# Encoder layer on one core: the modulation's later dot products run in the attention and beside the whole mLSTM, and pauses stand ahead of three TensorE steps

## The chip, the cores and the metric

The kernel runs on one core of a Trainium2 chip. The metric is the time of one execution on the device in microseconds (us); the profile takes one execution apart. TensorE (PE) multiplies matrices, VectorE (DVE), ScalarE (ACT) and GpSimd (POOL) work element by element, and SyncE (SP) issues nearly all DMA transfers. Every engine carries out its own instructions in the order in which they were written down, and waits at one whose inputs are not ready.

## The reference, cut to what matters

```python
cond = jax.nn.silu(c)                                        # (1, 1024)
mod = cond @ w_ada[l] + b_ada[l]                             # 6 x 1024
sh1, sc1, g1, sh2, sc2, g2 = jnp.split(mod, 6, axis=-1)
h = modulate(rms_norm(x, norm_mix_g[l]), sh1, sc1)           # h * (1 + sc1) + sh1
proj = h @ w_in[l]
q_a, k_a, v_a, qk_m, v_m, o_m, gates = jnp.split(proj, splits, axis=-1)
y_attn = axial_gqa_attention(q_a, k_a, v_a, ...)             # 8 heads of 64, 2 key/value heads, rotary
y_mem = bidirectional_mlstm(qk_m, v_m, o_m, gates, ...)      # 4 heads of 128, convolution of 5 taps ahead
mix = jnp.concatenate([y_attn, y_mem], axis=-1) @ w_out[l]
x = x + g1[:, None, :] * mix
h = modulate(rms_norm(x, norm_ffn_g[l]), sh2, sc2)
ffn = (jax.nn.silu(h @ w_gate[l]) * (h @ w_up[l])) @ w_down[l]
x = x + g2[:, None, :] * ffn
return rms_norm(x, final_norm_g)
```

All inputs are float32, the sequence has 1024 positions, the model 1024 channels, the FFN 2816. The modulation is a product of a vector with a 1024 x 6144 matrix of 24 MB. `sh1` and `sc1` are needed before the projection, `g1` (columns 16 to 23 of `mod`, 128 channels to a column) when the output projection is added to x, `sh2` and `sc2` (24 to 39) at the second norm, and `g2` (40 to 47) at the end of the FFN.

## The kernel before

Activations lie transposed, channels on the 128 partitions. Every large matmul is made of three (lines 298 to 300, `mm3`): weights and activations are split into a high part, rounded to fp32r by ScalarE (`whi`, `hh`), and the rest, made by GpSimd or VectorE (`wlo`, `hl`).

The kernel's own emitter fixes the order of the instructions. `Clock` holds an estimate of each engine's time. `Clock.chain` is a list of steps: each is written down when the one ahead of it should be done by that estimate, so the elementwise engines get their instructions in the order of estimated time. `Clock.streams` walks generators of TensorE work (`Stream`): the main ones go first, the filling ones (`un`, the units of the input projection or later of the output projection) when no main one is ready. TensorE itself never changes the order: a matmul that a chain writes down too early holds up everything behind it until its input is there. Elementwise instructions and DMA issues all go through one helper each (lines 96 and 303).

The stages, one after another:

- First norm and the first tiles of the projection, with the modulation's columns 0 to 15 as full dot products.
- The input projection's units (`IN`): `q_unit` (queries), `conv_unit` (mLSTM queries and keys with their convolution, tiles `xp` and `y`), `chunk_unit` (values, output gates and the mLSTM's gate columns). Beside them run `rope_steps` for the keys and four pairs of query heads, and `gate_steps`, a long chain on VectorE and ScalarE that turns the mLSTM's gates into cumulative sums, maxima and exponentials. Three of their steps are TensorE instructions written down by a chain: `squares` (lines 645 and 651: sums of squares of queries and keys, inputs `sqk` from ScalarE), `columns` (line 908: 16 transposes of the exponentials `T`, from ScalarE) and `spread` (line 922: a matmul that spreads the decay `dexp`, from VectorE, over all partitions). The stage goes on until the fourth pair of query heads is stored and the gates are done.
- Attention: three main streams (`scores`, line 978; `turned`, transposes of the probabilities, line 1010; `values`, line 1029) over 8 heads x 8 blocks of queries, filled with projection units.
- mLSTM: four main streams (`states`, `fronts`, `backs`, `ends`; tiles `mk`, `Cs`, `W`, `num`, `hs`), first filled with what is left of the input projection, then, from the loading of `x1` on, with the output projection (`MIX`). Between the two, the pool `big` and the projection's input are freed, and the tiles of x (`x1p`) take their place.
- Output projection, second norm, FFN.

The modulation's columns 16 to 47 are made late, in 64 half columns: `ada_late` loads one half column of the transposed `w_ada` (128 x 512, 256 KB, tile `ada`) and writes down one VectorE instruction that multiplies it by `cond` and sums along the row into `modacc`; the instruction that reads the sum out (`DVE_READ_ACCUMULATOR`) follows it. It has two buffers and asks for another one only when the one but last should be done by the emitter's estimate. It is called in three places: in the projection stage, at most once per estimated microsecond (`ready`), once ahead of every block of scores, both up to 48, and in the mLSTM (`ck.tick`, at every step of a stream) up to 64. `mod_sum` adds the two halves and the bias.

```python
        def ready():
            if ck.t > t_ada[0]:
                ada_late()
                t_ada[0] = ck.t + 1.0
            return rope_ok[3].done and gates_ok.done and not open_sum[0]
```

## Time and profile before

| | |
|---|---|
| median of 3 runs (lowest to highest) | 1405.2 us (1403.0 to 1405.35) |
| the profiled execution's own time | 1407.29 us |
| its span, first to last instruction | 1405.5 us |
| mean granted TensorE clock | 0.972 |
| busy: PE, DVE, ACT, POOL | 93%, 76%, 47%, 48% of the span |
| half columns on VectorE before 207 us, in 207 to 300, in 507 to 557 | 30, 18, 16 |
| scores of the attention begin; mLSTM's last output is stored | 206.8 us; 674.7 us |

How to read the profile. Times are in us from the span's start, mean durations of single instructions in ns. A line of waits reads: engine, tile and line that waited, the one that released it, us in total, times, longest. A line of stretches gives start and end, length, then busy us and number of instructions for PE, PEld (weight loads of TensorE), DVE, ACT and POOL, the granted TensorE clock (1.00 is full speed), the share of the 16 DMA engines that was busy, and GB/s. In a line of the timeline stand start, duration, engine, line, operation, output and inputs, and in square brackets the idle time ahead of it and what ended it. SPq is SP's own queue, in which DMA issues wait for their buffers. Tile names have no buffer numbers: `ada` is a half column, `T` both the gates' exponentials and the attention's transposed probabilities, `x` the residual stream.

### The profile page before, as it was taken

Reading aid. Unit: us, or ns where it says so; the run is one execution under the profiler, and the core shown is the slowest. Engines: PE = TensorE matmul, PEld = TensorE weight load, DVE = VectorE, ACT = ScalarE, POOL = GpSimd, SP = SyncE. Lnnn points to the kernel's source line nnn. Section 1 sums busy time; section 2 is a strip of 40 time slices with the busy share of each in tenths; the row PEclk is TensorE's granted clock in tenths of the full one; section 3 lists DMA queues with packets and bytes.
Section 4 is the critical chain, followed back from the end, with each engine's and each line's share of the span. In section 5 each row is a group of like instructions: output and inputs, shape, how many; then the busy total and the mean of one; then the engine's idle time right before and its main releaser. Section 6 shows DMA issues by size and latency. Waiting matters only on the chain.

```text
span 1405.5 us, 19481 instructions
## 1 busy us (share of the span) xinstructions
PE 1300.5 (93%) x6594; PEld 1072.1 (76%) x6602; DVE 1065.1 (76%) x1600; ACT 662.9 (47%) x1194; POOL 679.0 (48%) x555
## 2 busy tenths in 40 slices
PE   5789798999999989899996999999999999979997
PEld 2578577889878979777774888888888887757887
DVE  7947979986788848768589886666666654798866
ACT  5454316677666655454476333332332334344463
POOL 5555554545344336577421355454544545545542
PEclk9899989999999999999998999999999999989999
DMA  7446462322122146553552333322332259723324
GB/s 287 165 128 203 135 172 80 108 77 65 38 65 70 35 140 211 188 203 115 196 187 75 113 120 105 107 104 100 110 113 90 71 175 327 275 81 102 93 65 154
DMA packets 103172, 184.40 MB, mean 131 GB/s; under 512 B 11296, under 2 KB 32672, under 8 KB 103072
## 3 DMA queue, kind: packets, MB, share of 16 engines
q1 hardware_dynamic: 89968, 161.06, 36.0%
q10 hardware_dynamic: 13104, 22.10, 4.2%
q8 instruction: 52, 0.85, 0.2%
q14 instruction: 48, 0.39, 0.1%
HBM read 136.19 MB, written 43.25 MB: 128 GB/s over the span
## 4 chain that ended last, share of the span: by engine, by line
PE 61%; DVE 20%; DMA 6%; issue 5%; ACT 3%; POOL 3%; SPq 1%; DVEq 0%; ACTq 0%; POOLq 0%
PE acc L299 15%; PE acc L298 15%; PE acc L300 15%; DVE x L96 3%; PE av L1029 3%; DVE ada L96 3%; DVE sst L96 2%; PE T L1010 2%; DVE PT L96 2%; PE S L978 2%; DVE y L96 1%; PE acct L298 1%; PE acct L300 1%; PE acct L299 1%; DVE wd L96 1%
## 5 line engine op out<-in xcount | busy, mean ns | idle before, releaser
L96 POOL TENSOR_TENSOR wlo<-wst,whi 128x512 fp32r<-128x512 f32 (+2 forms) x196 | 279.5, 1432 | 285.0 <-ACT whi L96 272.9
L96 ACT ACTIVATE whi<-wst 128x512 fp32r<-128x512 f32 (+2 forms) x219 | 131.0, 605 | 125.1 <-POOL wlo L96 25.3
L96 POOL TENSOR_SCALAR P<-P,sst 128x1024 f32<-128x1024 f32 x64 | 88.9, 1392 | 141.1 <-DVE sst L96 106.4
L299 PE MATMUL acc<-x,whi 128*128 128x512 f32 x352 | 140.7, 400 | 5.9 <-DVE x L96 5.9
L96 POOL TENSOR_TENSOR wlo<-wr,whi 128x512 fp32r<-128x512 f32 x56 | 76.9, 1374 | 77.4 <-ACT whi L96 73.9
L298 PE MATMUL acc<-hh,whi 128*128 128x512 f32 x224 | 97.5, 435 | 14.1 <-ACT hh L96 11.8
L298 PE MATMUL acc<-whi,wch 128*128 128x512 f32 x244 | 97.2, 398 | 6.3 <-ACT wch L96 6.3
L96 ACT ACTIVATE P<-S,sst,colq 128x1024 f32<-128x1024 f32 x64 | 77.3, 1207 | 52.4 <-DVE sst L96 47.9
L299 PE MATMUL acc<-hl,whi 128*128 128x512 f32 x224 | 92.4, 412 | 8.2 <-POOL hl L96 4.5
L300 PE MATMUL acc<-whi,wcl 128*128 128x512 f32 x244 | 97.2, 398 | 2.9 <-DVE wcl L96 2.8
L299 PE MATMUL acc<-wlo,wch 128*128 128x512 f32 x244 | 97.0, 398 | 0.6 <-POOL wlo L96 0.5
L96 DVE SCALAR_TENSOR_TENSOR ada<-ada,cond 128x512 f32<-128x512 f32 (+1 forms) x79 | 80.2, 1023 | 18.3 <-DMA ada<-in_w_ada_dram 12.7
L300 PE MATMUL acc<-hh,wlo 128*128 128x512 f32 x224 | 91.5, 409 | 0.0
L96 DVE TENSOR_TENSOR sg<-acc,sg 128x512 f32<-128x512 f32 x67 | 45.4, 687 | 58.8 <-PE acc L300 58.5
L96 ACT ACTIVATE PT<-T 128x512 fp32r<-128x512 f32 x128 | 71.4, 597 | 37.7 <-PE T L1010 36.9
L96 ACT ACTIVATE whi<-wr 128x512 fp32r<-128x512 f32 x60 | 37.9, 632 | 108.1 <-DVE wr L96 50.3
L96 DVE TENSOR_TENSOR PT<-T,PT 128x512 fp32r<-128x512 f32 x128 | 82.8, 681 | 7.2 <-ACT PT L96 7.1
L96 POOL TENSOR_TENSOR wlo<-s,whi 128x512 fp32r<-128x512 f32 x40 | 53.8, 1347 | 70.7 <-ACT whi L96 70.7
L299 PEld LDWEIGHTS acc<-x,whi 128*128 128x128 f32 x352 | 67.0, 190 | 22.3 <-DVE x L96 7.3
L298 PE MATMUL acct<-whi,hh 128*128 128x256 f32 (+1 forms) x256 | 79.4, 310 | 2.5 <-ACT xp L96 1.2
L96 DVE TENSOR_TENSOR wcl<-wd,wch 128x512 fp32r<-128x512 f32 x50 | 48.0, 972 | 42.1 <-ACT wch L96 26.9
L1010 PE MATMUL T<-con,P 128*128 128x128 f32 x512 | 70.3, 275 | 10.2 <-DVE PT L96 7.4
(459 smaller groups left out, 3802.5 us busy)
## 6 DMA issues: line engine op xcount, KB each, us to landing
wr<-in_w_gu_dram SPq DMA_DIRECT2D x66, 256.0 KB, 2.8
ada<-in_w_ada_dram SPq DMA_DIRECT2D x64, 256.0 KB, 3.3
wd<-in_w_d_dram SPq DMA_DIRECT2D x22, 512.0 KB, 7.0
wst<-in_w_gu_dram SPq DMA_DIRECT2D x34, 256.0 KB, 3.1
wst<-act_d SPq DMA_DIRECT2D x33, 256.0 KB, 4.1
ada<-in_w_ada_dram SPq DMA_DIRECT2D x16, 512.0 KB, 5.5
wst<-in_w_o_dram SPq DMA_DIRECT2D x32, 256.0 KB, 4.3
act_d<-sg ACTq DMA_DIRECT2D x31, 256.0 KB, 2.0
```

The source lines that it names most:

```text
L96: return fn(*args, **kw)
L298: nc.tensor.matmul(acc, w[0], x[0], start=first, stop=False)
L299: nc.tensor.matmul(acc, w[0], x[1], start=False, stop=False)
L300: nc.tensor.matmul(acc, w[1], x[0], start=False, stop=last)
L978: nc.tensor.matmul(sp[:, halves(n)], qs[:, j * P:(j + 1) * P], k2[g][m][:, halves(n)], start=m == 0, stop=m == 1)
L1010: nc.tensor.transpose(tp[:, k], Pt[q][:, (4 * b + k) * P:(4 * b + k + 1) * P], ident)
L1029: nc.tensor.matmul(av, va[:, k, h // 4], PT[it][m][:, k], start=(k, m) == (0, 0), stop=(k, m) == (NJ - 1, 1))
```

## The change

The projection stage no longer calls `ada_late`. The attention makes 32 half columns (columns 16 to 31) instead of what was missing of 48. The mLSTM makes the other 32: until the input projection's end in the two buffers of the pool `big`, from then on, once the first tiles of the attention's output are split, in the ring `yat` of the mLSTM's pool (4 buffers, 2 asked for ahead); it goes on through the output projection's filling, and what is missing at the end is made in a closing loop. `cond` lies in the mLSTM's pool. `mod_sum` is called for 16 to 31 before the mLSTM and for 32 to 47, with `sc2`, when all are done. `later(dt)` is a step of a chain that writes nothing down and puts the steps after it off by `dt` us of the emitter's estimate: 2.5 us ahead of `squares`, 6 us ahead of `columns`, 5 us ahead of `spread`.

```diff
--- before.py
+++ after.py
@@ -617,6 +617,12 @@
         va_ok = [Flag(), Flag()]
         rp = []
 
+        def later(dt):
+
+            def wait():
+                ck.fin = ck.now + dt
+            return wait
+
         def rope_steps(i, accs):
 
             is_k = i == 4
@@ -676,7 +682,7 @@
                              lambda t=t, g=g: act.activation(k2[g][0], t, AF.Copy),
                              lambda t=t, g=g: gps.tensor_sub(k2[g][1], t, k2[g][0].bitcast(F32)), flag=k2_ok[g])
 
-            ck.chain(0.0, lambda: evac(0), lambda: evac(1), swap, squares)
+            ck.chain(0.0, lambda: evac(0), lambda: evac(1), swap, later(2.5), squares)
 
         def v_steps(accs):
             vt = bp.tile([P, S], F32, tag="big", name="vt")
@@ -925,26 +931,29 @@
 
             ck.chain(0.5, lambda: rows(0), lambda: rows(1), lambda: None, *[lambda i=i: soft(i) for i in range(3)], logf, mask,
                      *[lambda i=i: scan(i) for i in range(4)], ends, rows_r, rows_hl, inter,
-                     lambda: exps(0), lambda: exps(1), state, lambda: exps(2),
+                     lambda: exps(0), lambda: exps(1), state, lambda: exps(2), later(6.0),
                      *[lambda i=i, b=b: columns(i, b) for i in range(2) for b in range(2)],
-                     lambda: dve.tensor_scalar(cols[:, :, 1], cols[:, :, 1], QK, None, op0=OP.mult), decay, spread,
+                     lambda: dve.tensor_scalar(cols[:, :, 1], cols[:, :, 1], QK, None, op0=OP.mult), decay, later(5.0), spread,
                      lambda: None, flag=gates_ok)
 
         adas = []
         summed = []
 
-        def ada_late(last=48, ahead=2):
+        def ada_late(last=32, ahead=2):
 
             n = len(adas)
             if n == 64 and all(f.done for f in adas[-2:]) and not summed:
                 summed.append(1)
-                mod_sum(40, 48)
+                mod_sum(32, 48)
+                dve.scalar_tensor_tensor(sc2, mod[:, 32:40], 1.0, V("norm_ffn_g", 0, KT), op0=OP.add, op1=OP.mult)
             if n >= last or n >= ahead and not (adas[n - ahead].done and adas[n - ahead].t <= ck.t):
                 return
             j, i = 16 + n // 2, n % 2
-            t = PP["ada"].tile([P, HALF], F32, tag="ada", name="ada", bufs=ahead)
+            t = PP["ada_new"]()
             adas.append(ck.chain(dma(t, w_ada[j][:, halves(i)]), lambda: dve.scalar_tensor_tensor(
                 t, t, 1.0, PP["cond"][:, halves(i)], op0=OP.mult, op1=OP.mult, accum_out=modacc[:, i, j:j + 1])))
+
+        PP["ada_new"] = lambda: PP["ada"].tile([P, HALF], F32, tag="ada", name="ada", bufs=2)
 
 
         NQ = AH * NJ
@@ -1922,12 +1931,7 @@
             rp.append(stp.tile([P, S], F32, tag="x", name="rps", bufs=KT))
             dma(rp[i], rope[i])
 
-        t_ada = [0.0]
-
         def ready():
-            if ck.t > t_ada[0]:
-                ada_late()
-                t_ada[0] = ck.t + 1.0
             return rope_ok[3].done and gates_ok.done and not open_sum[0]
 
         ck.streams([un], stop=ready)
@@ -1939,7 +1943,7 @@
         att_q(0)
         ck.streams([Stream(values()), Stream(turned()), Stream(scores())], [un])
         ck.streams([un], stop=lambda: convs[-1].done and len(convs) == 8 and not open_sum[0])
-        while len(adas) < 48:
+        while len(adas) < 32:
             ck.need(*adas[-2:])
             ada_late()
         ck.need(*adas, *convs, *stores)
@@ -1947,28 +1951,26 @@
         appool.__exit__(None, None, None)
         kvpool.__exit__(None, None, None)
         bp = PP["ada"] = big_open(3)
-        load_cond(bp)
 
 
         def mod_sum(a, b):
             dve.tensor_add(mod[:, a:b], modacc[:, 0, a:b], V("b_ada", a, b - a))
             dve.tensor_add(mod[:, a:b], mod[:, a:b], modacc[:, 1, a:b])
 
-        mod_sum(16, 40)
+        mod_sum(16, 32)
         sc2 = const.tile([P, KT], F32, name="sc2")
-        dve.scalar_tensor_tensor(sc2, mod[:, 32:40], 1.0, V("norm_ffn_g", 0, KT), op0=OP.add, op1=OP.mult)
         mlpool = tc.tile_pool(name="ml", bufs=1)
         mp = mlpool.__enter__()
+        load_cond(mp)
         OPL[:] = mp, 4
         psum_open("ps2", {"acc": ("acc", 2), "acct": ("acc", 2), "tr": ("tr", 1), "U": ("U", 2), "E": ("E", 1),
                           "na": ("na", 1), "ni": ("ni", 1)})
         mem = [Stream(g) for g in (ends(), backs(), fronts(), all_states())]
         ck.tick = lambda: ada_late(64)
         ck.streams(mem, [un], stop=lambda: un.wait is None and all(f.done for v in vo_ok for f in v))
-        while not summed:
-            ck.need(*adas[-2:])
-            ada_late(64)
-        ck.tick = None
+        ck.need(*adas[-2:])
+        PP["ada_new"] = lambda: mp.tile([P, HALF], F32, tag="yat", name="ada", bufs=4)
+        ck.tick = lambda: (0, 0) in Y and all(y[2].done for y in Y[0, 0]) and ada_late(64)
         BIGP[0].__exit__(None, None, None)
         hTpool.__exit__(None, None, None)
         x1p = ctx.enter_context(tc.tile_pool(name="x1", bufs=1, side="right"))
@@ -1980,6 +1982,10 @@
                 ck.at(0.5 + 1.2 * (k + KT * n), lambda k=k, n=n: dma(new_x1(k, n, F32), xT[k][:, halves(n)]))
         ck.streams(mem, [un])
         ck.streams([un], stop=lambda: not open_sum[0])
+        while not summed:
+            ck.need(*adas[-2:])
+            ada_late(64)
+        ck.tick = None
         ck.need(*[f for ring in PP["ring"].values() for f in ring], *[f for y in ym_ok for f in y])
         mlpool.__exit__(None, None, None)
         midpool.__exit__(None, None, None)
```

## The prediction

> **What bounds the kernel now.** First the page: busy shares, then the slices.
>
> ```profile
> PE 1300.5 (93%) x6594; PEld 1072.1 (76%) x6602; DVE 1065.1 (76%) x1600; ACT 662.9 (47%) x1194; POOL 679.0 (48%) x555
> ...
> PE   5789798999999989899996999999999999979997
> ...
> PEclk9899989999999999999998999999999999989999
> ```
>
> TensorE is the bound: it is idle for 105 us of the 1405.5 us span, so an edit pays only by what it takes from TensorE's idle time or from stretches at a lower clock (the 8 of slice 6, 176 to 211 us), or costs by what it adds there. So I cut the span into the stages that the change touches.
>
> ```profile
> 120.00:207.00 87.00, 74.30 (x318) 59.49 (x316) 72.22 (x102) 30.46 (x44) 48.54 (x31) 0.90 0.56 173
> 207.00:300.00 93.00, 84.64 (x543) 72.99 (x542) 90.25 (x156) 60.24 (x102) 46.74 (x30) 1.00 0.35 104
> 300.00:360.00 60.00, 58.96 (x421) 53.44 (x420) 42.51 (x81) 41.99 (x76) 24.44 (x22) 1.00 0.18 53
> 360.00:507.00 147.00, 140.52 (x908) 122.57 (x907) 121.14 (x194) 94.84 (x166) 61.30 (x47) 1.00 0.16 48
> 507.00:557.00 50.00, 45.82 (x340) 43.07 (x343) 31.94 (x92) 26.00 (x69) 25.49 (x43) 1.00 0.70 215
> 557.00:601.00 44.00, 38.39 (x213) 32.54 (x214) 33.81 (x63) 19.89 (x53) 29.67 (x40) 0.92 0.62 208
> 585.00:607.00 22.00, 20.96 (x106) 16.62 (x106) 14.59 (x24) 11.65 (x30) 19.42 (x25) 1.00 1.02 361
> ```
>
> Columns: stretch, length, busy time of PE, PEld, DVE, ACT, POOL, granted clock, DMA share, GB/s. 120 to 207 is the gate and rotary stage beside the projection, 207 to 507 the attention, from 507 the mLSTM. The first row is the poorest: 12.7 us of TensorE idle and a clock of 0.90. The waits in it:
>
> ```profile
> PE T L922 <- DVE dexp L96: 4.7, 1, 4.7
> PE T L908 <- ACT T L96: 4.2, 2, 3.1
> PE ms L651 <- ACT sqk L96: 2.3, 2, 1.8
> PE acc L298 <- ACT xp L96: 1.5, 2, 0.7
> ```
>
> The first three are the steps that get a pause: spread (L922), columns (L908), squares (L651). TensorE stands in order at an instruction whose input ScalarE or VectorE has not finished. The clock:
>
> ```profile
> 136.00:144.00 8.00, 7.48 (x24) 6.16 (x24) 7.92 (x8) 2.18 (x5) 7.81 (x6) 0.57 0.33 99
> 150.00:160.00 10.00, 9.38 (x49) 7.59 (x47) 9.75 (x16) 3.05 (x5) 2.84 (x2) 1.00 0.42 127
> 174.00:185.00 11.00, 9.63 (x32) 8.34 (x33) 4.71 (x21) 0.19 (x2) 5.12 (x3) 0.53 0.60 168
> ```
> ```profile
> 151.84 1.84 PE L651 MATMUL ms<-con,sqk 128*128 128x2 f32 x16
> ...
> 175.95 3.57 PE L651 MATMUL ms<-con,sqk 128*128 128x2 f32 x16
> ```
>
> Right behind the squares' wait (about 135) and the spread's wait (to 175.4) the clock is low. The same 16 matmuls take 1.84 us at 151.84, where nothing was waited for, and 3.57 us behind the spread. Lost: 8 x 0.43 = 3.4 us, and 11 x 0.47 = 5.2 us less half of the 1.37 us in which TensorE was idle there anyway, 4.6 us. Together 8.0 us.
>
> **Where the dot products stand now.** VectorE's groups in 207 to 300 and in 512 to 557, then single tiles with their first and last start:
>
> ```profile
> L96 DVE SCALAR_TENSOR_TENSOR ada<-ada,cond 128x512 f32<-128x512 f32 x18 | 17.1, 950 | 0.1
> L96 DVE DVE_READ_ACCUMULATOR ada<-ada,cond 128x1 f32 x18 | 1.4, 80 | 0.0
> ```
> ```profile
> L96 DVE SCALAR_TENSOR_TENSOR ada<-ada,cond 128x512 f32<-128x512 f32 x16 | 12.7, 804 | 11.5 <-DMA ada<-in_w_ada_dram 6.0 <-DMA mq<-mqk_d 5.5
> L96 DVE DVE_READ_ACCUMULATOR ada<-ada,cond 128x1 f32 x16 | 1.3, 79 | 0.0
> ```
> ```profile
> L96 DVE SCALAR_TENSOR_TENSOR ada<-ada,cond x30: 654/682/2877, 96.6 to 200.1; 128x512 f32<-128x512 f32 x30
> ```
> ```profile
> L96 DVE SCALAR_TENSOR_TENSOR ada<-ada,cond x16: 677/684/1699, 512.8 to 556.3; 128x512 f32<-128x512 f32 x16
> ```
> ```profile
> L978 PE MATMUL S<-k,qs x79: 388/393/502, 206.8 to 298.8; 128*128 128x512 f32 x79
> ```
>
> There are 48 half columns before the mLSTM (30 up to 207, 18 up to 300) and 16 in it. One costs 1.03 us of VectorE in the attention (207 to 300), 0.88 us in the mLSTM (512 to 557). The rows with three durations (minimum, median, maximum in ns) give the 30 ahead of the attention, the 16 in the mLSTM, and the score matmuls, four to a block: 20 blocks in the stretch in which 18 products ran. Those ahead of the attention stand in the gate chain itself:
>
> ```profile
> 160.16 1.21 DVE L96 TENSOR_TENSOR Fr<-gB,mprev 64x1024 f32<-64x1024 f32 x1
> 161.30 0.68 DVE L96 SCALAR_TENSOR_TENSOR ada<-ada,cond 128x512 f32<-128x512 f32 x1
> ...
> 173.36 0.68 DVE L96 SCALAR_TENSOR_TENSOR ada<-ada,cond 128x512 f32<-128x512 f32 x1
> ...
> 174.07 1.15 DVE L96 TENSOR_SCALAR dexp<-rend,con 64x8 f32<-64x8 f32 x8
> ```
> ```profile
> SPq L303 <- DVE ada L96: 37.4, 18, 4.6
> ```
>
> The last row is SP's own queue in 120 to 215: 18 times it stood at an ada load whose buffer was still in use.
>
> **The change, part by part.**
>
> *Gate and rotary stage.* Removed: 30 dot products, 30 loads, and SP's 37.4 us at them. Behind those in SP's queue stood weight, rotary and query loads; TensorE shows no wait for weights, so that alone gives nothing, it only keeps the cover. Of the 30, those from 133 on lengthen the chain to dexp. Added: pauses of 2.5, 6.0 and 5.0 us, which hold no engine: the emitter places the three TensorE steps later, and projection matmuls fill the time. The waits to cover: 1.8 us at the squares' first stop (2.3 in all, the second 0.5); the columns 4.2 and spread 4.7, 8.9 together, against pauses of 6.0 + 5.0 and a chain that has lost several dot products of 0.76 us (0.68 + 0.08). All three should go: 11.2 us. With the stops gone the clock should hold, as it does at 151.84: 8.0 us. Upper end 19.2 us, lower end 11.2 us (the clock falls all the same). I take 17, near the upper end because both low stretches begin at a stop; 2 us go to what is late next, waits of the kind of the xp rows (0.7 each), met sooner. The pauses also put off the end of the gates; this stage goes on until the fourth query's rotary part is stored, so later gates move at most a half tile of projection from the attention's filling into this stage, dense TensorE work either way: nothing.
>
> *Attention.* 32 instead of 18. One is asked for ahead of each score block, and 18 in 20 blocks is that pace already, so 207 to 300 stays as it is and 14 more fall into 300 to 360: 14 x 1.03 = 14.4 us of VectorE, 42.5 becomes 57 of 60 us, or 53 at the median duration. TensorE's idle share was 9% where VectorE was 97% busy, 4.4% at 82%, 1.7% at 71% (the three attention rows). At about 93% I read 7%: 4.2 us for 1.0 now, so +3. Ends: 0 (hidden) and 14.4 (all on the path). The 14 loads share SP with the query loads, where a late one is part of that +3.
>
> VectorE's waits for the x loads in 557 to 601, for the next part:
>
> ```profile
> DVE x L96 <- DMA x<-in_xT_dram: 1.1, 2, 0.8
> ```
>
> *mLSTM.* 32 instead of 16. The first 16 run as before, one per 2.75 us (16 in 44 us). The other 16 follow at that pace, 557 to 601: 16 x 0.88 = 14.1 us, and VectorE has 10.2 us idle there: 3.9 us too much. Until the projection ends they keep the old two buffers, then they take the four y tiles, at which SP stands less. The switch waits for the two last ones ahead of the x loads, which lie in the freed space. Their loads meet the x loads: 585 to 607 runs at a DMA share of 1.02. Six loads of 0.26 MB at 361 GB/s are 4.4 us of lateness; VectorE's additions of x wait 1.1 us now, and two PSUM banks of filling cover most of the rest: I take a quarter, +1.1, and 3.9 + 1.1 = 5. The stretch also holds one accident of its own, seen from TensorE, VectorE and POOL:
>
> ```profile
> 568.62 1.20 PE L1814 MATMUL ni<-Cs,mq 128*128 128x260 f32 x2 [4.31 <-DVE num L96]
> ```
> ```profile
> 560.90 4.24 DVE L96 TENSOR_TENSOR hs<-hs,ss 128x512 f32<-128x512 f32 x1
> ```
> ```profile
> 560.84 3.76 POOL L96 TENSOR_TENSOR yal<-yat,yah 128x512 fp32r<-128x512 f32 x3
> ```
>
> A VectorE step of the size for which a dot product takes 0.68 us took 4.24 us beside three POOL steps, TensorE stopped 4.3 us, and the stretch's clock of 0.92 costs 44 x 0.08 = 3.5 us. Another order may lose all that. Term: +5; ends -7 (that accident gone, the rest hidden) and 14.1 + 4.4 + 3.5 = 22.
>
> [...]
>
> The stores of the mLSTM's outputs, first and last start, and the 64 loads of half columns with their time to landing:
>
> ```profile
> L303 SPq DMA_DIRECT2D ym_d<-ymt x8: 319/327/487, 555.1 to 674.7; - x8
> ```
> ```profile
> ada<-in_w_ada_dram SPq DMA_DIRECT2D x64, 256.0 KB, 3.3
> ```
>
> *The rest.* cond is loaded into the mLSTM's pool instead of the big pool, in the same place of the queue: 0. The sums over 16 columns instead of 24, and later over 16 instead of 8 with sc2, are a few VectorE steps of the size of the eight dexp steps (0.15 us each) whose result is needed only after the mLSTM's end: 0. The last products should be done by 601, and the mLSTM's last output is stored at about 675, so the closing loop waits for nothing; without that cover each would cost a load and a product, 3.3 + 0.9 us.
>
> **The sum.** The profiled execution took 1407.3 us (span 1405.5). -17 + 3 + 5 = -9: 1398.3. The median of the runs, 1405.2, lies 2.1 lower, so in its terms 1396.
>
> TensorE's waits for VectorE in 505 to 560, for rival 4:
>
> ```profile
> PE acct L298 <- DVE avt L96: 0.9, 1, 0.9
> ...
> PE tr L1875 <- DVE dn L96: 0.2, 1, 0.2
> ```
>
> **The rivals** (in median terms).
> 1. The clock stays low: the small squares and the transposes keep TensorE at little work even without stops. Only 11.2 comes back: 1405.2 - 11.2 + 8 = 1402. For it: the 133 to 138 stop was only 2.3 us and yet the clock fell; against it: 150 to 160 at 1.00. [...]
> 2. The mLSTM's accident goes too: 1405.2 - 17 + 3 - 7 = 1384. For it: it hangs on one meeting of two steps.
> 3. The gain comes back as a stop at the attention's start, whose query loads wait for the rotary steps' memory: with half of 17 kept, 1405.2 - 8.5 + 8 = 1405. Against it: these steps lose their dot products too.
> 4. Slower: from 557 to 601 VectorE is the bound, and every product there lies on TensorE's path, with two half-clock stretches of 3.4 us: 1405.2 - 17 + 3 + 14.1 + 6.8 = 1412. It decides from 14 us on in that place. For it: the clock of 0.92 and TensorE's 38.4 of 44 us there already; against it: in 505 to 560, with the same load of products, TensorE waited 1.1 us for VectorE in all.
>
> **How the numbers follow.** Forecast 0.5 (own range 1389 to 1402), rivals 0.13, 0.14, 0.11, 0.12. About 0.2%, 2.8 us, is what a measurement can tell here: faster is under 1402.4. Faster: nearly all of the forecast, rival 2, half of rival 1, a third of rival 3: 0.75. Same 0.13, slower 0.12. The range 1383 to 1408 leaves out rival 4 and a little below.
>
> **What would show it.** Right: no wait over 1 us at L651, L908, L922; a clock near 1.00 from 120 to the first scores, which begin some 17 us earlier than 206.8; 32 products up to about 360 less the gain; VectorE near 95% there; the rest done near 600. Wrong: a stop at the first scores, TensorE waiting for num, W or x between 550 and 610, or the clock low there.

## The result, and the profile after

The changed kernel takes 1414.4 us (median of 5 runs, 1410.38 to 1414.6), the kernel before 1405.35 us (1403.0 to 1407.94) beside it: ratio 1.0058, interval 1.0046 to 1.007. It is slower; 1396 was forecast, and the range ended at 1408. The profiled execution of the changed kernel is the quickest of its five (1410.38 us, span 1408.6), so its trace shows 3.1 us more span than that of before. The medians lie 9 us apart; what the other four executions lost beyond the traced one, about 4 us, no trace holds, and so the ledger below takes apart a third of the slowdown.

The page: busy time and slices.

```profile
PE 1300.8 (92%) x6602; PEld 1072.1 (76%) x6602; DVE 1065.3 (76%) x1600; ACT 663.4 (47%) x1194; POOL 684.7 (49%) x555
...
PE   5789979999999979899897899999999999989997
...
PEclk9899999999999989999999899999999999989999
```

The clock's 8 of slice 6 (176 to 211 us) is gone, and slice 15 (493 to 528 us, the mLSTM's start) has a 7 where before had an 8, and a clock of 8 where before had 9. Four stretches show it better, cut at each kernel's own milestones: the first scores, the attention's last value matmul, the last projection matmul that fills the mLSTM, the first matmul of the second norm. First after, then before, with the columns of the earlier stretch rows. (Before, the first score matmul starts at 205.6 us; the 206.8 us given ahead of the prediction is where the view that begins at 207 us first meets the scores.)

```profile
82.00:190.10 108.10, 105.65 (x576) 89.69 (x575) 67.07 (x78) 43.40 (x70) 63.25 (x38) 0.98 0.38 108
190.10:497.70 307.60, 288.11 (x1895) 252.56 (x1895) 266.79 (x457) 198.29 (x344) 134.10 (x100) 1.00 0.27 78
497.70:573.70 76.00, 63.92 (x436) 59.20 (x435) 51.05 (x136) 35.81 (x96) 39.48 (x58) 0.93 0.59 186
573.70:704.00 130.30, 114.97 (x547) 90.85 (x546) 92.61 (x186) 58.27 (x137) 89.38 (x99) 0.96 0.59 198
```
```profile
82.00:205.60 123.60, 110.90 (x573) 93.50 (x573) 92.44 (x139) 44.60 (x71) 60.76 (x38) 0.93 0.52 155
205.60:505.60 300.00, 285.05 (x1872) 249.84 (x1870) 254.61 (x428) 196.69 (x342) 133.88 (x99) 1.00 0.23 67
505.60:581.90 76.30, 66.68 (x468) 61.90 (x471) 51.94 (x135) 37.79 (x101) 38.87 (x59) 0.96 0.58 179
581.90:696.60 114.70, 108.33 (x531) 86.93 (x534) 80.78 (x154) 56.16 (x133) 83.90 (x98) 1.00 0.58 193
```

TensorE's work is the same in both kernels (busy 1300.5 us before, 1300.8 after), so the time is its work plus what is lost: idle time (length less PE busy) and low clock (length times what is missing to 1.00; the clock has two decimals, which leaves up to 0.7 us open in the three shorter stretches and 1.5 us in the attention). The ledger:

| us lost: idle + clock | before | after | change | forecast |
|---|---|---|---|---|
| 82 us to the first scores | 12.7 + 8.7 | 2.4 + 2.2 | -16.8 | -17 |
| attention | 14.9 + 0 | 19.5 + 0 | +4.6 | +3 |
| mLSTM up to the second norm | 16.0 + 3.1 | 27.4 + 10.5 | +18.8 | +5 |
| from there to the end | 30.7 + 14.6 | 28.6 + 12.9 | -3.8 | 0 |

They sum to +2.8 of the 3.1 us. The gain came as forecast and was lost in the mLSTM. The last row is scatter: over the experiments' kernels, which do the same there, that stretch loses 40 to 45 us.

Each figure is that of one trace. How far one trace can be trusted is shown by seven of the kernels below (after, `after_n2`, `after_n4`, `ghost_mlstm`, `ghost_n2`, `free_mlstm`, `free_n2`), whose traces hold the same instructions in the same order on TensorE, VectorE, ScalarE and GpSimd up to the attention's end, but for one step that clears `modacc` at the start of the last four. They lose 4.0 to 7.4 us ahead of the first scores; their attention takes 305.2 to 309.4 us and is idle for 16.8 to 19.5. A difference of 3 or 4 us between two traces is therefore not firm.

TensorE's waits from 120 us to the first scores after the change, and its longest in the mLSTM, first after, then before:

```profile
PE acc L298 <- ACT xp L96: 1.8, 2, 1.1
PE ms L657 <- ACT sqk L96: 0.7, 1, 0.7
```
```profile
PE ni L1823 <- DVE num L96: 11.1, 7, 2.7
PE na L1818 <- issue: 3.8, 1, 3.8
PE tr L1711 <- DMA mk<-mqk_d: 2.8, 1, 2.8
PE acc L298 <- ACT yah L96: 2.7, 1, 2.7
```
```profile
PE ni L1814 <- DVE num L96: 6.9, 4, 4.3
PE na L1809 <- ACT whi L96: 2.8, 1, 2.8
PE tr L1702 <- DMA mk<-mqk_d: 1.1, 1, 1.1
...
PE acc L298 <- ACT yah L96: 0.6, 1, 0.6
```

No single wait carries the mLSTM's loss. `ni` waits 4.2 us more for `num`, the first `na` 1.0, the first `tr` 1.7, and `yah`, the split of the mLSTM's last outputs, 2.1 us more than the 0.6 it waited before. (Lines are 6 to 9 later than before.)

### The profile page after: what moved, and what is told of

Its sections match the earlier page's. It is cut to its first block, busy times and chain, and to the rows that moved or that the text cites. A ratio compares the mean times of both kernels' runs of the same rounds, so it can differ in the third digit from the quotient of the medians.

```text
span 1408.6 us, 19465 instructions
## 1 busy us (share of the span) xinstructions
PE 1300.8 (92%) x6602; PEld 1072.1 (76%) x6602; DVE 1065.3 (76%) x1600; ACT 663.4 (47%) x1194; POOL 684.7 (49%) x555
## 4 chain that ended last, share of the span: by engine, by line
PE 56%; DVE 24%; issue 6%; DMA 5%; ACT 4%; POOL 3%; SPq 1%; ACTq 0%; DVEq 0%; POOLq 0%
PE acc L299 14%; PE acc L300 14%; PE acc L298 14%; DVE sst L96 4%; DVE x L96 3%; DVE ada L96 3%; DVE y L96 3%; DVE PT L96 3%; PE av L1038 2%; PE T L1019 2%; PE acct L298 1%; PE acct L300 1%; PE acct L299 1%; PE S L987 1%; DVE Cs L96 1%
## 5 line engine op out<-in xcount | busy, mean ns | idle before, releaser
L298 PE MATMUL acc<-hh,whi 128*128 128x512 f32 x224 | 96.0, 429 | 12.9 <-ACT hh L96 9.8
L96 DVE SCALAR_TENSOR_TENSOR ada<-ada,cond 128x512 f32<-128x512 f32 (+1 forms) x79 | 80.7, 1027 | 10.5 <-ACT cond L96 8.5
L96 ACT ACTIVATE whi<-wr 128x512 fp32r<-128x512 f32 x60 | 37.9, 632 | 106.5 <-DVE wr L96 50.0
L1019 PE MATMUL T<-con,P 128*128 128x128 f32 x512 | 70.1, 275 | 11.9 <-DVE PT L96 9.3
```

The lines of the kernel that those rows point to most:

```text
L96: return fn(*args, **kw)
L298: nc.tensor.matmul(acc, w[0], x[0], start=first, stop=False)
L1019: nc.tensor.transpose(tp[:, k], Pt[q][:, (4 * b + k) * P:(4 * b + k + 1) * P], ident)
```

## The experiments

Times are medians, with the ratio to the kernel before on the same chip and its interval. "Loss" is always the ledger's third row, idle time plus clock, 19.1 before and 37.9 after.

**Each half alone.** `pauses_only`: the kernel before with the three `later(...)` steps. `moves_only`: the changed kernel without them.

> The kernel before with the three pauses alone; all dot products stay where they were. Theory A (the stops at the squares, columns and spread come from steps written down too early; the pauses cure them, whoever else is on VectorE): the 12.7 us of TensorE idle and the 8 us of low clock between 120 and 207 us mostly go, the first scores come some 15 us earlier than 205.6, and as attention and mLSTM keep their order the whole time falls by about 15 us, to some 1390. Theory B (the dot products in the gate chain keep it late, so that pauses alone cover only part): the first scores come at most 8 us earlier, the time is 1397 to 1402. Rival C (time won ahead of the attention is given back in it, because VectorE sets its pace): the first scores early, the time within 4 us of 1405.

> The changed kernel without the three pauses: only the dot products are moved. Theory A: the stops stay for the larger part, since TensorE still stands at steps written down too early; some 5 to 12 us slower than the changed kernel's 1414. Theory B: the moved products were what made the chain late, so the stops shrink to under 4 us in all and the time is within 4 us of the changed kernel.

`pauses_only` took 1402.8 us (0.9976, 0.996 to 0.9992), `moves_only` 1418.4 (1.0086, 1.0068 to 1.0103). TensorE's waits from 120 us to the first scores in `pauses_only`, and the longest of `moves_only`:

```profile
PE acc L298 <- ACT xp L96: 4.2, 2, 2.3
PE ms L657 <- ACT sqk L96: 2.3, 2, 1.1
PE T L829 <- DVE gI L96: 2.1, 2, 1.6
```
```profile
PE ms L657 <- ACT sqk L96: 6.2, 1, 6.2
```

The waits at columns and spread are gone with either half. But while products stand in the chain the pauses bring other waits (`xp`, `gI`), and without pauses the squares wait 6.2 us at one place. First scores begin at 201.8 us with pauses, 196.1 with the moves, 190.1 with both: loss ahead of them 17.1, 13.4, 4.6 for 21.4 before. The 17.1 is not firm: `pauses_n1` below has the same instructions up to the mLSTM and lost 21.0, first scores at 205.3. The 4.6 is: the fourteen kernels here that have the pauses and no product in the projection stage lose 3.8 to 7.4. So the two halves are one edit: alone the pauses give 0 to 4 us, the moves 8, together 14 to 18. Of the theories, `pauses_only` fits theory B (scores 3.8 us earlier, time a little above its 1402), and `moves_only` lies between its two: 4.0 us slower than the changed kernel, but with 6.2 us left at the squares alone. The losing part is the moves: `moves_only` has a loss of 33.9 in the mLSTM, `pauses_only` 18.4.

**The attention.** `att48`: pauses, nothing in the projection stage, 48 products in the attention and 16 in the mLSTM as before. `ghost_att`: the changed kernel, 14 of the attention's 32 left out but charged to the emitter's clock. `drop_att`: `att48` with the 48 left out and not charged. `gap`: pauses, products in the projection stage only outside the gate chain, the rest of 48 in the attention.

```diff
+            if 18 <= n < 32:          # ghost_att
+                adas.append(ck.chain(ck.dma(P * HALF * 4, 0.5), lambda: ck.run("dve", 0.595)))
+                return
```

> Pauses, no dot product in the projection stage, 48 in the attention (one ahead of each of 48 blocks of scores), 16 in the mLSTM as in the kernel before, its code unchanged. If the loss of the changed kernel lies in the mLSTM's 16 extra products (theory M): the mLSTM takes 169 us as before, the attention some 5 us more than the changed kernel's 307.6, the time is about 1398. If the attention's extra products cost in full (theory N, about 1 us each on the path): the attention takes over 320 us and the time stays above 1408.

> The changed kernel, but products 19 to 32 of the attention are neither loaded nor multiplied, only charged, so that every other instruction keeps its place. Leaves out 14 half columns. Theory P for the attention (VectorE sets its pace where it is over 95% busy, so a product costs most of its duration): the attention falls from 307.6 us by 5 to 9. Theory O (the order, or the emptier projection stage, made it longer): under 3 us. The mLSTM after it stays at 184 either way.

> The kernel before with the pauses, with the 48 half columns ahead of the mLSTM left out altogether, so that no product runs or is charged in the projection stage or in the attention; 16 in the mLSTM. If the attention's growth of 7.6 us is due to its 14 added products, it falls to 295 to 299 us (300.0 with 18 before), first scores at about 190, the time at about 1385. If the growth goes with the earlier start (less of the projection is done by then, and more is left to fill), it stays at 304 or more, and the time at about 1393.

> The whole computation: pauses; the projection stage makes dot products only ahead of the gate chain and behind its end, some 12 of the 30; the attention makes the others up to 48; mLSTM and everything after it as in the kernel before. If keeping products out of the gate chain is what wins time there: first scores at 191 to 195 us against 205.6; the attention some 8 us longer, the mLSTM 169 us, the time about 1398. If the attention takes back more than its filling gives: within 3 us of 1405.

| | products in the attention | length | idle | time (ratio, interval) |
|---|---|---|---|---|
| before | 18, start 205.6 | 300.0 | 14.9 | |
| `drop_att` | 0, start 189.9 | 300.5 | 11.9 | 1397.0 (0.9937, 0.9917 to 0.9957) |
| after | 32, start 190.1 | 307.6 | 19.5 | 1414.4 |
| `ghost_att` | 18 and 14 charged only, 189.7 | 305.6 | 14.7 | 1410.4 (1.0033, 1.0019 to 1.0047) |
| `att48` | 48, start 190.1 | 313.8 | 20.9 | 1404.8 (0.9993, 0.9979 to 1.0007) |
| `gap` | the rest of 48, start 197.7 | 312.2 | 20.1 | 1408.6 (1.0022, 1.0006 to 1.0038) |

At the early start the idle time grows from 11.9 to 19.5 (16.8 to 19.5 in the seven traces) to 20.9 us with 0, 32, 48 products, 0.1 to 0.2 us each. The length grows by more, since other filling falls into it, which is work TensorE must do anyway. `drop_att` met neither expectation: 300.5 us with no product at all, where before had 300.0 with 18, so the early start seems to lengthen the attention by itself. `ghost_att` is 2.0 us shorter than the changed kernel, as its theory O says, but 305.6 us lies inside the seven traces' 305.2 to 309.4, and its clock was 0.98: what 14 products cost there is not shown. `att48` has theory M's attention (313.8 us) and mLSTM (168.0 us to the last stored output), but the time stays 7 us above M's 1398. `gap` has a short mLSTM (166.0 us, 169 expected), but its scores begin later than the 191 to 195 us expected, its attention is 12 us longer than before, and it is 3 us slower than before. Nothing here is lost on the scale of the mLSTM. In `ghost_att` all 32 of the mLSTM remain, and its loss there is 42.4 us.

**The mLSTM, work and charge.** `drop16` and `free_mlstm` leave out the last 16 half columns, neither loaded nor charged (`drop16` in the order and pools of before, `free_mlstm` in those of after). `ghost_mlstm` leaves the same 16 out, but charges them to the emitter's clock (condition `n >= 48` in the lines above). `uncharged` does all, and charges none of the late ones; a load counts as 3.5 us, and the mLSTM's first products multiply by `cond` ahead of its silu. `att48_uncharged` is that edit on `att48`. `ghosts_before` is the kernel before with 16 more that are only charged, in the mLSTM.

```diff
-            adas.append(ck.chain(dma(t, w_ada[j][:, halves(i)]), lambda: dve.scalar_tensor_tensor(
+            nc.sync.dma_start(t, w_ada[j][:, halves(i)])        # uncharged
+            adas.append(ck.chain(3.5, lambda: nc.vector.scalar_tensor_tensor(
```

> Pauses, no dot product in the projection stage, 32 in the attention, then the mLSTM in the code of the kernel before, with its 16; the 16 half columns between are left out. Theory P (the mLSTM is paced by its own chain over VectorE, GpSimd and ScalarE, not by TensorE; 16 more products, done or only charged in the emitter, lengthen it): the mLSTM (last attention matmul to last stored output) takes 169 us as in the kernel before, the attention about 307 as in the changed kernel, the time about 1396. Theory Q (the mLSTM is slower because the attention leaves it in another phase, with other filling): it takes over 176 us, the time stays above 1402.

> The changed kernel's own code, but the last 16 half columns are neither loaded, multiplied nor charged in the emitter's clock (left out). Theory P: the mLSTM falls from 184.4 us to about 170, where the charged ghosts still took 180.6, and the time to about 1397. If cond's new place, the switch or the x loads' start slow it (theory R): over 176 us in spite of that, and slower than the kernel with the old mLSTM code and the same products.

> The changed kernel, but of the 32 half columns in the mLSTM the last 16 are neither loaded nor multiplied; the emitter's clock is charged as if they were, so that all other instructions stand in the same order. Leaves out 16 half columns of the modulation. Theory M (the 16 extra products and loads cost by their work on VectorE and the DMA queues): the stretch from the projection's end to the mLSTM's end shrinks from 108.6 us by 10 or more towards the 93.1 before, the time is about 1400. Theory O (the new order of the mLSTM's instructions costs, not the work): within 4 us of the changed kernel's 1414.

> The changed kernel, whole, except that the emitter's clock is not charged for the late half columns (neither load nor product; a load is taken to be 3.5 us late). Theory A (the charge of about 0.6 us a product spreads the mLSTM's own steps): the mLSTM takes 174 to 178 us (184.4 in the changed kernel), the attention about 305, the time is about 1403 to 1405. Theory B (the products' work on VectorE itself makes the mLSTM longer): the mLSTM stays at 182 us or more, with TensorE waiting longer at num and tr, and the time at 1410 or more.

> 48 half columns in the attention and 16 in the mLSTM as in the run att48 (attention 313.8 us, mLSTM 168.0, 1404.8 us), with the emitter's clock not charged for them. Theory A: the attention falls to 308 to 311 us, the mLSTM stays at 168, the time is about 1400 to 1402. Theory B: the attention stays at 313 or more and the time at 1404 to 1406.

> The kernel before, whole, with 16 more half columns that are only charged to the emitter's clock in the mLSTM, neither loaded nor multiplied. Theory A: the mLSTM grows from 169 to between 176 and 181 us though no instruction is added, and the time is 1412 to 1416. Theory B: nothing is added to any engine, so 169 us and 1404 to 1407.

| | products in the mLSTM | loss there | time (ratio, interval) |
|---|---|---|---|
| `drop16` | 16 | 25.7 | 1403.2 (0.9985, 0.9971 to 1.0) |
| `free_mlstm` | 16 | 27.5 | 1403.0 (0.9967, 0.995 to 0.9984) |
| `ghost_mlstm` | 16, and 16 charged only | 35.4 | 1406.4 (1.0005, 0.9993 to 1.0017) |
| `uncharged` | 32, none charged | 30.1 | 1415.8 (1.0082, 1.006 to 1.0105) |
| `att48_uncharged` | 16, none charged | 33.2 | 1415.7 (1.0078, 1.0057 to 1.0099) |
| `ghosts_before` | 16, and 16 charged only | 18.6 | 1409.9 (1.0023, 1.0004 to 1.0041) |

The loss is that of the mLSTM in one execution, the time that of the whole kernel in the median of many, and the two do not agree on the split between work and charge. (Differences of times are taken from the ratios to the kernel before; each of these is uncertain by 2 to 3 us.)

*Work.* In the traces of `ghost_mlstm` and of the changed kernel TensorE, ScalarE and GpSimd carry out the same instructions in the same order; only 16 loads and products differ. By loss they cost 2.5 us (35.4 to 37.9), but the changed kernel's trace is the quickest of its five executions; by time they cost 7 us (1.0005 to 1.0058).

*Charge.* `free_mlstm` and `ghost_mlstm` do the same work, in the same order on TensorE up to 556 us and in another from there on. The charge, which moves all later steps, costs 7.9 us by loss (27.5 to 35.4) and 5 by time (0.9967 to 1.0005). In the order of before it adds no loss in the mLSTM (`ghosts_before`, 18.6 for 19.1; its extra time lies ahead of the mLSTM, first scores at 207.3, attention 302.4 us).

*No charge at all* is worse: the attention takes 313.8 us in `uncharged` for 307.6, 320.5 in `att48_uncharged` for 313.8. A likely reason, not tested, is that the emitter then writes TensorE's steps down too early. These two kernels have another order from the attention on, so they give no price for the work.

Against the expectations, with the mLSTM counted from the attention's end to its last stored output: `drop16` (171.4 us) and `free_mlstm` (172.3) come near theory P's length, but their times lie 6 to 7 us above its forecasts. `ghost_mlstm` is 8 us quicker than the changed kernel, between its two theories. `uncharged` (178.6 us) has about theory A's length and theory B's time, `ghosts_before` (167.2 us) theory B's length and a time between the two, and `att48_uncharged` fits neither. The theory that the charge as such makes the loss fell with these. A price that is 7.9 in one order and -0.5 in another points to the order, which the next runs put to the test.

**The order by itself.** One line ahead of the mLSTM's streams puts the emitter's estimate later and changes nothing else:

```diff
+        ck.until(ck.t + 2.0)
         mem = [Stream(g) for g in (ends(), backs(), fronts(), all_states())]
```

`after_n2` and `after_n4` are the changed kernel with 2 and 4 us, `pauses_n1` and `att48_n1` those kernels with 1 us, `ghost_n2` and `free_n2` the two mLSTM runs above with 2 us.

> The changed kernel, whole, with one line more: at the mLSTM's start the emitter's estimate is put 2 us later, so that the same steps are written down in another order. In the changed kernel the mLSTM's two stretches (end of the attention to the second norm) lost 37.9 us to TensorE's idle time and clock, before 19.1. Order theory (the loss is an accident of the order that the estimate gives): it falls by 5 us or more, towards 20 to 32 us, and the time to 1397 to 1409. Product theory (32 products in the mLSTM cost this much in any order): it stays at 34 to 41 us, the time at 1408 to 1416.

> The same with 4 us instead of 2. Order theory: the loss differs from that of the 2 us run and from 37.9 by several us, anywhere in 20 to 40 us. Product theory: 34 to 41 us again.

> The run of the pauses alone (16 products in the mLSTM, loss 18.4 us there, time 1402.8) with the emitter's estimate 1 us later at the mLSTM's start. Order theory: the 18.4 of before and of the pauses alone was a good draw, and another order gives 22 to 30 us and a time of 1406 to 1414. Product theory: 16 products cost what they did, 17 to 21 us, and the time stays at 1401 to 1405.

> The run att48 (48 half columns in the attention, 16 in the mLSTM, loss 27.2 us there, time 1404.8) with the emitter's estimate 1 us later at the mLSTM's start. Order theory: the loss moves by several us either way, 18 to 32, and with a better draw the time falls to 1397. Product theory: 25 to 29 us, 1403 to 1407.

> The run ghost_mlstm (the last 16 half columns left out, neither loaded nor multiplied, but charged to the emitter's clock) with the emitter's estimate 2 us later at the mLSTM's start, as in after_n2. Charge theory (the emitter spreads the mLSTM's other steps, and that makes the loss): loss of idle time and clock from the attention's end to the second norm 32 to 38 us, as with all 32 done (33.7 to 39.6), time 1404 to 1408. Work theory (the loss comes from the products themselves on VectorE and the queue): 22 to 29 us, as in the runs with 16, time 1396 to 1402.

> The run free_mlstm (the last 16 half columns left out and not charged) with the emitter's estimate 2 us later at the mLSTM's start. Both theories: a loss in the band of the runs with 16 products, 22 to 29 us, and a time of 1398 to 1404; if it comes out above 31, 16 and 32 products are not told apart by this measure at all.

The mLSTM in one stretch each, from the attention's end to the second norm, in the order of the table's rows (the loss in the table is worked out in two stretches, as in the ledger, and differs from these rows by up to 1 us of rounded clock):

```profile
497.70:704.00 206.30, 178.89 (x981) 150.05 (x980) 143.66 (x321) 94.08 (x233) 128.86 (x156) 0.95 0.59 193
```
```profile
500.70:703.50 202.80, 177.98 (x981) 148.45 (x980) 147.80 (x320) 94.76 (x233) 126.41 (x156) 0.96 0.61 197
```
```profile
500.70:710.50 209.80, 178.59 (x981) 148.90 (x980) 146.10 (x320) 94.16 (x233) 127.10 (x156) 0.96 0.59 190
```
```profile
497.90:698.20 200.30, 177.53 (x974) 150.16 (x981) 136.21 (x288) 94.84 (x233) 123.50 (x156) 0.96 0.55 178
```
```profile
498.80:694.30 195.50, 174.83 (x974) 148.90 (x981) 135.06 (x288) 94.28 (x233) 122.36 (x156) 0.97 0.56 183
```
```profile
505.70:702.80 197.10, 177.20 (x1005) 150.71 (x1004) 131.68 (x288) 94.31 (x234) 122.67 (x156) 0.97 0.56 182
```
```profile
505.00:693.30 188.30, 168.91 (x946) 142.00 (x945) 129.34 (x288) 93.60 (x232) 123.02 (x156) 0.97 0.57 186
```

| | loss as it was | loss with the shift | time (ratio, interval) |
|---|---|---|---|
| after | 37.9 | | 1414.4 |
| `after_n2` | | 33.7 | 1409.4 (1.0022, 1.0004 to 1.004) |
| `after_n4` | | 39.6 | 1419.4 (1.0092, 1.0066 to 1.0118) |
| `ghost_n2` | 35.4 | 31.5 | 1403.6 (0.9985, 0.9973 to 0.9998) |
| `free_n2` | 27.5 | 27.2 | 1403.2 (0.9987, 0.9972 to 1.0002) |
| `pauses_n1` | 18.4 | 25.1 | 1409.4 (1.0026, 1.001 to 1.0042) |
| `att48_n1` | 27.2 | 25.1 | 1402.5 (0.9974, 0.9958 to 0.9991) |

The traces show the same instructions in the same order up to the mLSTM's start, and another order from there. With not one instruction more, the loss moves by between 4.2 us less and 6.7 us more, and the time by up to 7 (`pauses_only` to `pauses_n1`) and by 10 between the two shifts of the changed kernel. Run by run: `pauses_n1` is what the order theory foresaw (22 to 30 us, 1406 to 1414), `after_n4` stays in the product theory's 34 to 41, though its time lies above, `after_n2` falls by 4.2 us, between the two, and `att48_n1` stays in the product theory's loss. So neither theory holds alone. With 16 products done and the emitter knowing of them, the loss is 18.4, 18.6 and 19.1 us in three orders (`pauses_only`, `ghosts_before`, before) and 23.9 (`gap`) to 29.1 (`drop_att`) in eight others: the kernel before had a good draw. With 32, done or charged, it is 31.5 to 42.4 in seven orders, and 30.1 in `uncharged`. (`att48_uncharged` lost 33.2 with 16 that the emitter does not know of.) The bands do not overlap but for `ghosts_before`, and each is 5 to 11 us wide. Why the three low orders are good stays open: they share the 30 late products ahead of the attention and first scores after 201 us, but `pauses_n1` shares these too and lost 25.1.

At equal shift, the work costs 2.2 us by loss (`ghost_n2` 31.5, `after_n2` 33.7) and 5 by time (0.9985 to 1.0022), the charge 4.3 by loss (`free_n2` 27.2, `ghost_n2` 31.5) and nothing by time (0.9987 to 0.9985). By loss `ghost_n2` lies half a microsecond from the charge theory's 32 to 38 and 2.5 from the work theory's 22 to 29, while its time, 1403.6, lies between the two. `free_n2` came as expected.

So 16 more half columns in the mLSTM cost, work and charge together, 10.4 and 6.5 us by loss and 13 and 5 by time in the two orders. How this splits is open: the work is 2 to 3 us by the traces and 5 to 7 by the times.

`att48_n1` (1402.5 us) and `pauses_only` (1402.8) are the quickest kernels that do the whole computation, and not told apart. Of the whole kernels that ran in more than one order, only `att48` is at or below the kernel before in both (1404.8 and 1402.5).

## Why the prediction was wrong

*Bound.* That an edit pays only through TensorE's idle time and its clock held: the ledger in these terms sums to the span's change within 0.3 us.

*Gate and rotary stage, -17.* Right, and for its reasons: no wait over 1 us at the squares, columns and spread, a clock of 0.98 and 15.5 us earlier scores; idle 10.3 us less (11.2 forecast) and clock 6.5 (8.0 forecast). The reserve of 2 us for waits of the `xp` kind was in place too (1.8 us). (In the forecast's sum, 5.2 less half of 1.37 is 4.5 and not 4.6, which changes nothing.) What the text did not see is that neither half does it alone. Rival 1 showed only in small: with no wait over 1.1 us left, the clock was 1.00 from 130 to 160 us, with squares at 136.87 and 153.35 us and transposes for the columns from 158.65. Behind the squares at 163.33 us, which had waited 0.66 us, it was 0.57 from 165 to 169 us; that cost 1.7 us of the 2.2 that this stretch still lost to the clock.

*Attention, +3.* Measured +4.6, and +1.9 to +4.6 of idle time in the seven traces. Products came at the pace forecast, the 32nd at 341 us. But VectorE was busy only 83% in the place where 93% to 95% was foreseen (300 to 360 us before, 283 to 350 now, second row), and TensorE's idle time grew there by 2.4 of the 4.6 us. The size is right, the share from which it was read was not reached.

The same four places as in the prediction's rows, some 17 us earlier in the attention and 9 in the mLSTM:

```profile
190.00:283.00 93.00, 83.37 (x530) 71.76 (x528) 90.02 (x156) 58.27 (x98) 45.12 (x31) 1.00 0.38 110
283.00:350.00 67.00, 63.56 (x446) 57.32 (x445) 55.69 (x111) 44.64 (x80) 29.08 (x24) 1.00 0.36 103
...
498.00:548.00 50.00, 41.99 (x275) 38.89 (x275) 27.35 (x80) 22.25 (x60) 21.78 (x40) 0.90 0.61 192
548.00:592.00 44.00, 36.74 (x234) 31.81 (x232) 37.95 (x84) 20.79 (x53) 31.15 (x35) 1.00 0.72 235
```

*mLSTM, +5: the step that failed.* Measured +18.8, inside its ends of -7 to 22 but far from the value taken. It was worked out as "16 x 0.88 = 14.1 us, and VectorE has 10.2 us idle there: 3.9 us too much", plus 1.1 for the x loads. The overload did not exist: VectorE was busy 38.0 us of the 44 in the fourth row, where the sum gives 33.8 + 14.1 = 47.9. Only 12 products stood there, not 16; the last 15 ran from 564.6 to 627.1 us, one per 4.5 us and not per 2.75. From 553 to 629 us a product took 0.79 us in the mean, 0.87 with the step that reads the sum out, as the sum had it:

```profile
L96 DVE SCALAR_TENSOR_TENSOR ada<-ada,cond 128x512 f32<-128x512 f32 x17 | 13.3, 789 | 0.6 <-DMA ada<-in_w_ada_dram 0.6
```

What failed is the sentence beside it, "The first 16 run as before", and with it the idea that everything else keeps its place. From 498 to 548 us TensorE idled 8.0 us for 4.2 in the same place before, and the clock was 0.90 for 1.00, though 17 products had run by 554.4 us for 16 by 556.3. With the same 16 products and no charge for more (`free_mlstm`), the loss in the mLSTM is already 8.4 us above that of before. By time, the forecast without its +5 is 14 us under before, and `free_mlstm` is 5 under it: 9 us were lost with none of the added products, by the traces most of it in the mLSTM. The other kernels with 16 products and an earlier start show the like: 23.9 to 29.1 us for 19.1. The added 16 then cost 10.4 us by loss and 13 by time, and 6.5 and 5 in the shifted order, for the 5 forecast.

The account of it is this: every charged product, and the earlier start, move the mLSTM's chains in the emitter's order, and TensorE, in order, then stands at steps whose inputs are late. That the order alone moves the loss by several us is shown by the shifts; that it accounts for all of the 18.8 is argued, and the split between order and work is open. The range failed because the order's scatter was only given to one accident (-7 if it went) and not as an uncertainty on either side.

*The rivals.* Rival 4 has the outcome's sign and nearly its size (1412), but not its mechanism: VectorE was busy 86% in that place and the clock there was 1.00. Its sign did show, TensorE waiting for `num`, 5.7 us from 550 to 610 us, but 4.3 us of that were there before. Rival 2's accident did not go away, a like one stands at 645 us for that at 560. Three views of the changed kernel, TensorE, VectorE and POOL:

```profile
651.98 0.68 PE L1823 MATMUL ni<-Cs,mq 128*128 128x260 f32 x2 [2.21 <-DVE num L96]
```
```profile
647.54 3.77 DVE L96 SCALAR_TENSOR_TENSOR Cs<-Cs,dec 128x130 f32<-128x130 f32 x4
```
```profile
645.61 3.89 POOL L96 TENSOR_TENSOR yal<-yat,yah 128x512 fp32r<-128x512 f32 x3
```

Four `Cs` steps, 0.34 us each where no POOL step runs beside them (565.20 and 609.86 us), take 3.77 us beside three POOL steps, and `num`, queued behind them on VectorE, comes late. The products paid little for such meetings: 0.79 us in the mean, for the 0.68 of one with no POOL step beside it (610.12 us), is some 2 us over 17. Rival 3 did not occur: the scores began 15.5 us earlier.

*The rest, 0.* `cond` in the mLSTM's pool did no harm that the runs show. VectorE stood 8.55 us at the first product until `cond` was ready, but its next step after two products waited for TensorE anyway:

```profile
507.70 0.69 DVE L96 SCALAR_TENSOR_TENSOR ada<-ada,cond 128x512 f32<-128x512 f32 x1 [8.55 <-ACT cond L96]
...
513.28 0.35 DVE L96 SCALAR_TENSOR_TENSOR Cs<-Cs,dec,U 128x130 f32<-128x130 f32 x1 [4.27 <-PE U L1739]
```

And `drop_att`, with the old place, has the waits at `mk` and `na` too: 2.0 and 4.6 us. The closing loop waited for nothing; the last product ran at 627 us, not near 600.

## What to carry to other kernels

Where a planner writes down the order, moving work changes the order of everything behind it, and that can cost more than the work: here a kernel with none of the added products already lost 8.4 of the 18.8 us. Before a change of 1% is believed, or its loss, a few orders are to be drawn on purpose (one line that shifts the estimate), since one order is one draw with a scatter of several microseconds (here from 4.2 us less to 6.7 us more loss); and a split of a few microseconds that is read from single traces is to be held against the medians of the times, which here gave another one. A ledger of TensorE's idle time and clock, stage by stage between milestones, shows at once which term of a forecast failed.

## What the runs showed of the hardware

- Some VectorE steps took much longer beside GpSimd steps: a 128x130 `Cs` step that takes 0.34 us alone took 0.94 in the mean in the rows above. The two `num` steps just ahead of these (647.01 us), which read one input from PSUM (`ni`), took 0.60 us together beside the same row of POOL steps, as two do later without them (0.61 at 653.12 us). A product can meet POOL too: the one at 515.57 us took 1.61 us, amid three `wlo` steps (514.14 to 518.30 us); `W` stood behind it on VectorE, and TensorE's stop of 3.79 us ahead of the first `na` ended at 517.62, half a microsecond after `W` began.
- The clock fell behind short stops. In the changed kernel TensorE had 2.69 us of idle time from 506 to 509 (one wait of 2.79 us) and was at 0.67 right after; behind the next stop, of 2.62 us in the row and 3.79 us in all, at 0.50:

```profile
506.00:509.00 3.00, 0.31 (x3) 0.10 (x1) 1.29 (x4) 1.93 (x3) 0.00 (x0) 1.00 1.04 338
509.00:512.00 3.00, 2.42 (x11) 2.07 (x12) 0.01 (x2) 1.66 (x3) 1.42 (x4) 0.67 1.09 381
512.00:515.00 3.00, 1.84 (x6) 1.18 (x5) 0.35 (x1) 2.99 (x9) 2.30 (x6) 0.76 0.62 227
515.00:518.00 3.00, 0.38 (x2) 0.41 (x3) 2.70 (x6) 0.27 (x2) 3.00 (x3) 0.81 0.00 0
518.00:521.00 3.00, 3.00 (x15) 2.84 (x15) 1.21 (x4) 1.53 (x5) 2.16 (x5) 0.50 0.74 227
```

- Executions with the same instructions up to a place arrive there at different times: the first scores at 190.1, 192.7 and 191.3 us in after, `after_n2` and `after_n4`, at 201.8 and 205.3 in `pauses_only` and `pauses_n1`. A gain of 3 us read from one trace is within that.
